# Output projection in two halves, with the next mix maximum's product between them

## The chip, the cores and the metric

The kernel runs on one core of a Trainium2 chip. The metric is the device time of one execution in microseconds (us), lower is better. TensorE (PE) multiplies matrices and has a row of its own for loading weights (PEld), VectorE is DVE, ScalarE is ACT, GpSimd is POOL, and SyncE (SP) issues most of the transfers.

## What is computed

The reference is a backbone of two layers over 2048 latent tokens and 256 context tokens of 1024 features. Each layer makes `mix_x`, the gated outputs of three groups of heads, and then projects it:

```
x_new = x + gate_x[:, None, :] * (mix_x @ w_out[l])
...
ctx = ctx + gate_c * (mix_c @ w_out[l])      # first layer only
x = x_new
...
return rmsnorm(x, norm_f)
```

Each layer begins with an RMSNorm of `x` that is scaled and shifted. The kernel does that of the second layer inside the projection of the first, tile by tile; inside the projection of the second layer it does the final RMSNorm. The change touches only the output projections.

## The kernel before, in words

`mix` lies in device memory. The function `outproj` goes over tiles of 128 tokens, from the last to the first: 18 tiles in the first layer (t from 17 to 0), 16 in the second (t from 15 to 0). A tile is multiplied with `w_out` in float16 pairs: each operand is split into a high part and a low remainder, which makes 24 products for each half of the 1024 outputs, so 48 matmuls of 512 columns per tile (`out_mm`). They go into two PSUM banks, `b_pj` and `b_a`.

To be split, a tile of mix needs its largest absolute value. That takes a chain over four engines:

- `fetch`: SP issues the transfer of the tile into `mx` (two buffers).
- `prep`: DVE takes the maximum along each row (`ms<-mx`), ACT puts it on a diagonal (`dg<-ident,ms`).
- `prepb`: PE multiplies `ones` with that diagonal into a bank `b_b` (`top_b`), so that all partitions see all row maxima. I call it the maximum's product.
- `prep2`: DVE reduces the bank and makes the scale (four short instructions on `ms`), and ACT writes the high part (`m<-mx,ms`; the tile `m2` has two buffers).
- `prep3`: DVE writes the low part (`m<-mx,ms,m`).

What comes out of PSUM goes through `evac` (DVE multiplies the two banks with scale and gate into `xn`, POOL adds `xt`, SP stores the result in the first layer), and through `finish`: ACT sums the squares, POOL makes the power (`rst`), DVE scales (`xh` in the first layer, the output in the second). In the first layer every second tile ends with `put`: PE transposes two tiles of `xh` into banks `b_b` and `b_c`, and ACT, DVE and POOL write the result as `hu` and, split in high and low, as `hx`, the input of the next layer. Also in the first layer, twelve of the steps carry one of four `hooks` that get a block of the next layer's weights ready: load it, take its maximum (DVE, 2.28 us), make its own product on PE, split it (ACT and DVE). `put` stands at the end of the steps t = 15, 13, 11, ... 1, hooks at t = 15, 14, 13, 11, 10, 9, 7, 6, 5, 3, 2, 1.

Every engine but SP runs its part in the order in which the code records it: the class `Pin` (whose line 72 stands for all such instructions in the profile) keeps that order. SP's order is made by a scheduler. So the order of one step of the loop in `outproj` is the order on PE, DVE, ACT and POOL; an instruction that waits holds up all that stand behind it on its engine.

Of the kernel before, what the change touches and what calls it, by code (L numbers as in the profile page):

```python
# [77 lines left out]
def body(ctx: ExitStack, tc: tile.TileContext, a, out, dbg=None):  # L78
    nc = tc.nc
    V, S, G, TE = nc.vector, nc.scalar, nc.gpsimd, nc.tensor  # L80

    def sb(name, bufs=1, side="left"):
        return tc.tile_pool(name=name, bufs=bufs, reuse_waits="tile", side=side)
# [7 lines left out]
    def bank(tag):  # L91
        return ps.tile([P, 512], F32, tag=tag, name="b_" + tag)
# [115 lines left out]
    def rms(pool, xt, junk, S=S, G=G):  # L208
        st = pool.tile([P, 4], F32, tag="rst", name="rst")
        S.activation(out=junk, in_=xt, func=AF.Square, accum_out=st[:, 0:1])  # L210
        G.tensor_scalar(out=st[:, 1:2], in0=st[:, 0:1], scalar1=1.0 / DM, scalar2=EPS, op0=ALU.mult, op1=ALU.add)
        G.tensor_tensor(out=st[:, 2:3], in0=st[:, 1:2], in1=neghalf[:, 0:1], op=ALU.pow)
        return st[:, 2:3]
# [14 lines left out]
    def put_e(pool, l, tiles, pts, V=V, S=S, G=G, hook=None):  # L228
        w2 = 0 if tiles[0] < NL else 1
        t0 = min(tiles) * P  # L230
        for g, pt in enumerate(pts):
            u = pool.tile([P, 2, 256], F32, tag="hu", name="hu", bufs=3)
            for q in range(2):
                kb = 2 * g + q
                src = pt[:, q * 256:(q + 1) * 256]
                if q == 0 or g in PE_A:
                    S.activation(out=u[:, q, :], in_=src, func=AF.Identity, scale=modA[l][:, w2, kb:kb + 1], bias=modS[l][:, w2, kb:kb + 1])
                else:
                    V.tensor_scalar(out=u[:, q, :], in0=src, scalar1=modA[l][:, w2, kb:kb + 1], scalar2=modS[l][:, w2, kb:kb + 1], op0=ALU.mult, op1=ALU.add)
            ks = slice(2 * g, 2 * g + 2)  # L240
            V.tensor_copy(hx[:, 0, ks, t0:t0 + 256], u)
            (G if g < 3 else V).tensor_tensor(out=hx[:, 1, ks, t0:t0 + 256], in0=u, in1=hx[:, 0, ks, t0:t0 + 256], op=ALU.subtract)
            if hook:
                hook(g)
# [1306 lines left out]

        return fetch, prep, prepb, prep2, prep3

    def out_mm(w, t, ms, m2, te=TE):
        pts = [bank("pj"), bank("a")]
        n = 3 * KB
        terms = [(k, mi, wi) for k in range(KB) for mi, wi in ((0, 0), (0, 1), (1, 0))]
        order = [(i, hf) for i in range(n) for hf in range(2)] if t else [(i, hf) for hf in range(2) for i in range(n)]
        for i, hf in order:
            k, mi, wi = terms[i]  # L1560
            te.matmul(out=pts[hf], lhsT=m2[:, mi, k, :], rhs=w[:, wi, k, hf * 512:(hf + 1) * 512], start=(i == 0), stop=(i == n - 1))
        return t, ms, pts

    def outproj(l, last, xin, w, hooks, mid, fetch, prep, prepb, prep2, prep3, ready, mx, done):
        with ExitStack() as st:
            kp = st.enter_context(sb("ok", 1, "right"))
            wk = st.enter_context(sb("owk", 2, "right"))
            gts = kp.tile([P, 2, DM], F32, name="gts")
            nc.sync.dma_start(out=gts.rearrange("p a n -> p (a n)"), in_=gated[l].rearrange("a b -> (a b)").unsqueeze(0).to_broadcast([P, 2 * DM]))
            if last:  # L1570
                nf = kp.tile([P, DM], F32, name="nf")
                nc.sync.dma_start(out=nf, in_=a["norm_f"][0:1, :].to_broadcast([P, DM]))
            held = []
            v, s, g, te = (Pin(tc, e) for e in (V, S, G, TE))

            def fetch_x(t):
                xt = wk.tile([P, DM], F32, tag="xt", name="xt", bufs=4 if last else 3)
                nc.sync.dma_start(out=xt, in_=xin(t))
                return xt

            def evac(t, ms, pts, xt):
                gi = 0 if t < NL else 1
                fast = last and t == 0
                xn = wk.tile([P, DM], F32, tag="xn", name="xn", bufs=3)
                sp = wk.tile([P, 4], F32, tag="sp", name="sp")
                for hf in range(2):
                    sl = slice(hf * 512, (hf + 1) * 512)
                    v.scalar_tensor_tensor(out=xn[:, sl], in0=pts[hf], scalar=ms[:, 4:5], in1=gts[:, gi, sl], op0=ALU.mult, op1=ALU.mult)
                    (v if fast else g).tensor_tensor(out=xn[:, sl], in0=xn[:, sl], in1=xt[:, sl], op=ALU.add)
                    if fast:  # L1590
                        s.activation(out=xt[:, sl], in_=xn[:, sl], func=AF.Square, accum_out=sp[:, hf:hf + 1])
                        v.tensor_tensor(out=xn[:, sl], in0=xn[:, sl], in1=nf[:, sl], op=ALU.mult)
                if not last:
                    nc.sync.dma_start(out=xres[t * P:(t + 1) * P, :], in_=xn)
                return t, xt, xn, sp

            def finish(t, xt, xn, sp):
                if last and t == 0:
                    g.tensor_tensor(out=sp[:, 2:3], in0=sp[:, 0:1], in1=sp[:, 1:2], op=ALU.add)
                    g.tensor_scalar(out=sp[:, 2:3], in0=sp[:, 2:3], scalar1=1.0 / DM, scalar2=EPS, op0=ALU.mult, op1=ALU.add)  # L1600
                    g.tensor_tensor(out=sp[:, 3:4], in0=sp[:, 2:3], in1=neghalf[:, 0:1], op=ALU.pow)
                    r = sp[:, 3:4]
                else:
                    r = rms(wk, xn, xt, S=s, G=g)
                if not last:
                    xh = wk.tile([P, DM], F32, tag="xh", name="xh")
                    v.tensor_scalar_mul(xh, xn, r)
                    held.append((t, xh))
                elif t == 0:
                    v.tensor_scalar_mul(xt[:, 0:512], xn[:, 0:512], r)  # L1610
                    s.activation(out=xt[:, 512:DM], in_=xn[:, 512:DM], func=AF.Copy, scale=r)
                    for sl in (slice(0, 512), slice(512, DM)):
                        nc.sync.dma_start(out=out[t * P:(t + 1) * P, sl], in_=xt[:, sl])
                else:
                    v.scalar_tensor_tensor(out=xt, in0=xn, scalar=r, in1=nf, op0=ALU.mult, op1=ALU.mult)
                    nc.sync.dma_start(out=out[t * P:(t + 1) * P, :], in_=xt)

            def put():
                if len(held) == 2:
                    tiles = [z[0] for z in held]  # L1620
                    put_e(wk, l + 1, tiles, put_t(tiles, [z[1] for z in held], te=te), V=v, S=s, G=g)
                    held.clear()

            ready = [ready]
            prev = None
            for t in range(done[0], -1, -1):
                xt = fetch_x(t)
                cur = out_mm(w, *ready.pop(0), te=te) if prev else done
                if prev:
                    prev = evac(*prev)  # L1630
                if t > 1:
                    z = prep(*mx, V=v, S=s)
                    if t > 2:
                        mx = fetch(t - 3)
                if prev:
                    finish(*prev)
                if t > 1:
                    z = prep2(*prepb(*z, te=te), V=v, S=s)
                if hooks and t < done[0] and t % 4:
                    hooks.pop(0)()  # L1640
                put()
                if t > 1:
                    ready.append(prep3(*z, V=v))
                prev = *cur, xt
            mid()
            finish(*evac(*prev))
            put()

    def xin0(t):
# [7 lines left out]
    with sb("s0", 2, "right") as s0:  # L1657
# [10 lines left out]
        v, s, g, te = (Pin(tc, e) for e in (V, S, G, TE))  # L1668
# [13 lines left out]
        def fetch(i):  # L1682
            if i < len(pairs):
                xs[i] = xt = s0.tile([P, 2, DM], F32, tag="xt", name="xt", bufs=3)
                for q in range(2):
                    tc.keep_in_program_order(nc.sync.dma_start(out=xt[:, q, :], in_=xin0(pairs[i] + q)))
# [25 lines left out]
        pts = []  # L1712
# [35 lines left out]
    for l in range(2):  # L1748
# [56 lines left out]
        v, s = Pin(tc, V), Pin(tc, S)  # L1805
# [12 lines left out]
        def mid():  # L1818
            wst.close()
            if not last:  # L1820
                fst[0] = ExitStack()
                ug[0] = four_pool(fst[0])
                for b in (3, 2):
                    four_x(ug[0], b, nw["fx"])
# [161 lines left out]
```

## Time and profile before

| | |
|---|---|
| median of 3 runs | 2532.82 us (2531.42 to 2536.8) |
| the profiled execution | 2537.43 us, its span 2535.6 us |
| busy share of the span: PE, DVE, ACT, POOL | 92%, 63%, 44%, 44% |
| mean granted clock of TensorE | 0.967 |

A busy share is a mean over the whole span, and the matmuls' records overlap. What the projections cost is read from the stretches in which they run: 1152 to 1386 us for the first layer and 2355 to 2532 us for the second.

### The profile page before, as it was taken

Reading aid. Unit: us, or ns where it says so; the run is one execution under the profiler, and the core shown is the slowest. Engines: PE = TensorE matmul, PEld = TensorE weight load, DVE = VectorE, ACT = ScalarE, POOL = GpSimd, SP = SyncE. Lnnn points to the kernel's source line nnn. Section 1 sums busy time; section 2 is a strip of 40 time slices with the busy share of each in tenths; the row PEclk is TensorE's granted clock in tenths of the full one; section 3 lists DMA queues with packets and bytes.
Section 4 is the critical chain, followed back from the end, with each engine's and each line's share of the span. In section 5 each row is a group of like instructions: output and inputs, shape, how many; then the busy total and the mean of one; then the engine's idle time right before and its main releaser. Section 6 shows DMA issues by size and latency. Waiting matters only on the chain. (4 is left out here: it accounts for less than half of the span.)

```text
span 2535.6 us, 44432 instructions
## 1 busy us (share of the span) xinstructions
PE 2333.9 (92%) x16878; PEld 1554.5 (61%) x16878; DVE 1609.2 (63%) x3607; ACT 1126.5 (44%) x2049; POOL 1117.4 (44%) x1303
## 2 busy tenths in 40 slices
PE   5989998999978999999889999999999699999998
PEld 3555454454546999895444554555555589989444
DVE  5765666666865666695665435667666566669554
ACT  3523554555555444342333224666656434444222
POOL 1534444455544444453334234555555444445232
PEclk7999999999989999999999999999999899999999
DMA  6304124124222100364433021141221210126442
GB/s 250 117 3 131 60 83 123 49 86 121 88 62 66 44 34 35 102 191 154 138 121 110 31 67 49 54 105 55 62 64 34 72 36 35 38 80 200 154 150 100
DMA packets 128298, 225.16 MB, mean 89 GB/s; under 512 B 18346, under 2 KB 81444, under 8 KB 122452
## 3 DMA queue, kind: packets, MB, share of 16 engines
q1 hardware_dynamic: 122900, 212.68, 24.9%
q0 software_dynamic: 5184, 9.64, 2.6%
q8 instruction: 133, 2.18, 0.4%
q14 instruction: 81, 0.66, 0.1%
HBM read 176.89 MB, written 51.47 MB: 90 GB/s over the span
## 5 line engine op out<-in xcount | busy, mean ns | idle before, releaser
L72 PE MATMUL b_pj<-hx,w 128*128 128x512 f16 (+1 forms) x3168 | 690.7, 365 | 0.9 <-DVE w L72 0.9
L72 POOL TENSOR_TENSOR pl<-pt,ph 128x512 f16<-128x512 f32 (+6 forms) x300 | 307.5, 1026 | 433.8 <-ACT ph L72 365.7
L72 PEld LDWEIGHTS <-w 128*128 128x128 f16 x3168 | 305.8, 99 | 276.6 <-issue 15.0
L72 PEld LDWEIGHTS <-hx 128*128 128x128 f16 x5088 | 440.5, 100 | 11.0 <-issue 4.7
L72 PE MATMUL b_pj<-w,hx 128*128 128x192 f16 (+2 forms) x4272 | 396.9, 252 | 4.5 <-DVE zt L72 4.5
L72 PE MATMUL b_pj<-wo,m 128*128 128x512 f16 x816 | 306.2, 384 | 0.0
L72 PE MATMUL b_a<-wo,m 128*128 128x512 f16 x816 | 305.7, 384 | 0.0
L72 PEld LDWEIGHTS <-m 128*128 128x128 f16 x1632 | 161.8, 99 | 190.4 <-issue 9.0
L72 DVE SCALAR_TENSOR_TENSOR pt<-b_a,sc,TS 128x160 f32<-128x160 f32 (+4 forms) x432 | 153.1, 400 | 154.4 <-PE b_a L72 113.6
L72 ACT ACTIVATE pt<-pt,psh 128x480 f32<-128x480 f32 (+1 forms) x192 | 121.7, 634 | 168.2 <-DVE pt L72 158.1
L72 PE MATMUL b_c<-ph,vt 128*128 128x320 f16 (+5 forms) x888 | 179.2, 295 | 0.9 <-ACT ph L72 0.9
L72 PEld LDWEIGHTS <-vt 128*128 128x128 f16 x1332 | 120.8, 100 | 86.2 <-issue 23.2
L72 ACT CAST ph<-pt 128x512 f16<-128x512 f32 (+6 forms) x300 | 166.5, 555 | 9.5
L72 POOL TENSOR_TENSOR xn<-xn,xt 128x512 f32<-128x512 f32 x66 | 82.4, 1270 | 178.0 <-DVE xn L72 178.0
L72 PE MATMUL b_a<-Q,K 128*128 128x320 f16 (+5 forms) x444 | 120.9, 295 | 10.4 <-ACT Q L72 10.2
L72 PE MATMUL b_c<-pl,vt 128*128 128x320 f16 (+5 forms) x444 | 126.9, 295 | 3.6 <-POOL pl L72 3.6
L72 PE MATMUL b_a<-q,k 128*128 128x320 f16 (+5 forms) x444 | 121.6, 295 | 3.5 <-DVE MX L72 1.8
L72 DVE CUSTOM_DVE_ANT_0 b_b<-b_b,tmi 128x512 f32<-128x512 f32 (+3 forms) x144 | 86.5, 601 | 60.0 <-PE b_b L72 58.8
L72 ACT ACTIVATE pt<-b_a,psh,sc 128x512 f32<-128x512 f32 (+1 forms) x108 | 81.0, 750 | 67.1 <-PE b_a L72 61.8
L72 POOL TENSOR_TENSOR hx<-hu,hx 128x512 f16<-128x512 f32 x54 | 69.5, 1302 | 72.6 <-DVE hx L72 72.2
L72 POOL TENSOR_TENSOR ats<-ATm 128x512 f32<-128x512 f32 x34 | 43.3, 1274 | 129.0 <-DVE ATm L72 129.0
L72 PEld LDWEIGHTS <-q 128*128 128x128 f16 x540 | 51.5, 98 | 79.1 <-issue 24.1
(271 smaller groups left out, 4262.7 us busy)
## 6 DMA issues: line engine op xcount, KB each, us to landing
mx<-mixd SPq DMA_DIRECT2D x34, 512.0 KB
ws<-in_w_in SPq DMA_DIRECT2D x16, 1024.0 KB
xt<-in_x SPq DMA_DIRECT2D x32, 512.0 KB
ws<-in_w_ada SPq DMA_DIRECT2D x16, 1024.0 KB
ws<-in_w_out SPq DMA_DIRECT2D x16, 1024.0 KB
TS<-in_ts SPq DMA_DIRECT2D x12, 1000.0 KB
xres<-xn SPq DMA_DIRECT2D x18, 512.0 KB
qdt_d<-qkT SPq DMA_DIRECT2D x34, 256.0 KB
```

Of the source, the lines that this page charges most:

```text
L72: return self.tc.keep_in_program_order(f(*args, **kw))
```

## The change

`out_mm` can now hand back its second 24 matmuls as a function. In a step of `outproj` PE records the first 24, then the maximum's product, then the second 24; before, all 48 stood ahead of the product. The low part of a tile of mix is written one step later, behind `evac` and the row maximum of that step, and the fetch into the freed `mx` buffer follows it. The squares and the power of a norm (`norm_r`) are recorded ahead of the product's reduction, and the scaling (`finish`) behind the second 24 matmuls.

```diff
-    def out_mm(w, t, ms, m2, te=TE):
+    def out_mm(w, t, ms, m2, te=TE, split=False):
         pts = [bank("pj"), bank("a")]
         n = 3 * KB
         terms = [(k, mi, wi) for k in range(KB) for mi, wi in ((0, 0), (0, 1), (1, 0))]
         order = [(i, hf) for i in range(n) for hf in range(2)] if t else [(i, hf) for hf in range(2) for i in range(n)]
-        for i, hf in order:
-            k, mi, wi = terms[i]
-            te.matmul(out=pts[hf], lhsT=m2[:, mi, k, :], rhs=w[:, wi, k, hf * 512:(hf + 1) * 512], start=(i == 0), stop=(i == n - 1))
+        def half(z):
+            for i, hf in order[z * n:(z + 1) * n]:
+                k, mi, wi = terms[i]
+                te.matmul(out=pts[hf], lhsT=m2[:, mi, k, :], rhs=w[:, wi, k, hf * 512:(hf + 1) * 512], start=(i == 0), stop=(i == n - 1))
+
+        half(0)
+        if split:
+            return (t, ms, pts), lambda: half(1)
+        half(1)
         return t, ms, pts
...
-            def finish(t, xt, xn, sp):
+            def norm_r(t, xt, xn, sp):
...
                 else:
                     r = rms(wk, xn, xt, S=s, G=g)
+                return t, xt, xn, r
+
+            def finish(t, xt, xn, r):
...
             ready = [ready]
-            prev = None
+            prev = late = None
             for t in range(done[0], -1, -1):
                 xt = fetch_x(t)
-                cur = out_mm(w, *ready.pop(0), te=te) if prev else done
                 if prev:
+                    cur, more = out_mm(w, *ready.pop(0), te=te, split=True)
                     prev = evac(*prev)
+                else:
+                    cur, more = done, lambda: None
                 if t > 1:
                     z = prep(*mx, V=v, S=s)
-                    if t > 2:
-                        mx = fetch(t - 3)
+                if late:
+                    ready.append(prep3(*late, V=v))
+                    late = None
+                if t > 2:
+                    mx = fetch(t - 3)
+                if prev:
+                    prev = norm_r(*prev)
+                if t > 1:
+                    z = prepb(*z, te=te)
+                more()
+                if t > 1:
+                    late = prep2(*z, V=v, S=s)
                 if prev:
                     finish(*prev)
-                if t > 1:
-                    z = prep2(*prepb(*z, te=te), V=v, S=s)
                 if hooks and t < done[0] and t % 4:
                     hooks.pop(0)()
                 put()
-                if t > 1:
-                    ready.append(prep3(*z, V=v))
                 prev = *cur, xt
             mid()
-            finish(*evac(*prev))
+            finish(*norm_r(*evac(*prev)))
             put()
```

On PE, inside the matmuls of the first layer's tile 16 (`m_12966` is its split mix, `b_b<-dg,ones` the product of a later tile's maximum):

```order
 L72 LDWEIGHTS m_12966
 L72 MATMUL b_a<-wo,m_12966 128x512
+L72 MATMUL b_b<-dg,ones 128x128
 L72 LDWEIGHTS m_12966
 L72 MATMUL b_pj<-wo,m_12966 128x512
```

The product now stands between the tile's 24th and 25th matmul; before, the same row stood behind the 48th.

On DVE, from the end of the first `put` of the first layer (`hx<-hu,hx` is its last instruction) to the reduction of the next product:

```order
 L72 CAST hx<-hu 128x2x256 x2
 L72 TENSOR_TENSOR hx<-hu,hx 128x2x256
-L72 SCALAR_TENSOR_TENSOR m_13645<-mx,ms,m_13645 128x1024
-L72 SCALAR_TENSOR_TENSOR xn<-b_pj,ms,gts 128x512
-L72 SCALAR_TENSOR_TENSOR xn<-b_a,ms,gts 128x512
-L72 TENSOR_REDUCE ms<-mx 128x1
+L72 SCALAR_TENSOR_TENSOR xn<-b_pj,ms,gts 128x512
+L72 SCALAR_TENSOR_TENSOR xn<-b_a,ms,gts 128x512
+L72 TENSOR_REDUCE ms<-mx 128x1
+L72 SCALAR_TENSOR_TENSOR m_13643<-mx,ms,m_13643 128x1024
+L72 TENSOR_REDUCE ms<-b_b 128x1
+L72 TENSOR_SCALAR ms<-ms 128x1
```

The low part of mix moved from ahead of the two evacuations and the row maximum to behind them; `put` stands ahead of both, before and now.

On SP, at the first steps of the first layer's projection (`xres<-xn` is the store of `evac`, `mx` the fetch of a tile of mix, `xt` that of the residual):

```order
+L1600 DMA xres<-xn 128x1024
 L1527 DMA mx<-mixd_88 128x8x128
-L1594 DMA xres<-xn 128x1024
-L1578 DMA xt<-in_x 128x1024 x2
+L1584 DMA xt<-in_x 128x1024
+L1600 DMA xres<-xn 128x1024
 L1527 DMA mx<-mixd_88 128x8x128
```

The store, which waits for POOL, now stands ahead of the fetch of mix in each step.

## Rows read from the trace of the kernel before

**Rows 1.** Waits of the weight loads, first layer's projection: waited for, total us, times, longest

```profile
PEld b_b L72 <- ACT dg L72: 13.3, 6, 4.6
...
PEld b_b L72 <- DVE xh L72: 4.5, 2, 2.9
PEld b_b L72 <- DVE ms L72: 4.1, 2, 2.5
```

**Rows 2.** Waits of PE for a maximum's diagonal, second layer's projection

```profile
PE b_b L72 <- ACT dg L72: 0.9, 1, 0.9
```

**Rows 3.** Windows, the seven from 1187.3 to 1372.2 us: their sum

```profile
sum 184.90, PE 168.90 PEld 85.50 DVE 113.96 ACT 62.27 POOL 71.15; mean PE 24.13 PEld 12.21 DVE 16.28 ACT 8.89 POOL 10.16
```

**Rows 4.** Timeline of weight loads, first layer: start, us, tile, count [idle before <- releaser]

```profile
1176.73 0.41 PEld L72 LDWEIGHTS b_b<-dg,ones 128*128 128x128 f32 x2
...
1187.31 0.41 PEld L72 LDWEIGHTS b_b<-dg,ones 128*128 128x128 f32 x2
1187.63 0.47 PEld L72 LDWEIGHTS b_b<-ident,xh 128*128 128x128 f32 x4
...
1189.38 10.13 PEld L72 LDWEIGHTS <-m 128*128 128x128 f16 x48
1200.05 0.30 PEld L72 LDWEIGHTS b_b<-dg,ones 128*128 128x128 f32 x2 [0.54 <-ACT dg L72]
...
1213.65 0.42 PEld L72 LDWEIGHTS b_b<-ident,xh 128*128 128x128 f32 x4 [2.49 <-DVE ms L72]
...
1254.64 0.30 PEld L72 LDWEIGHTS b_b<-dg,ones 128*128 128x128 f32 x2 [4.58 <-ACT dg L72]
...
1361.49 0.52 PEld L72 LDWEIGHTS b_b<-dg,ones 128*128 128x128 f32 x4 [1.96 <-ACT dg L72]
```

**Rows 5.** Timeline of DVE around the first put

```profile
1187.94 0.29 DVE L72 TENSOR_REDUCE ms<-b_b 128x1 f32<-128x128 f32 x1 [1.21 <-PE b_b L72]
...
1190.43 0.54 DVE L72 TENSOR_SCALAR hu<-b_b,modA,modS 128x256 f32<-128x256 f32 x1 [1.75 <-ACT hu L72]
...
1195.85 1.27 DVE L72 SCALAR_TENSOR_TENSOR m<-mx,ms,m 128x1024 f16<-128x1024 f32 x1
1197.04 0.74 DVE L72 SCALAR_TENSOR_TENSOR xn<-b_pj,ms,gts 128x512 f32<-128x512 f32 x1
...
1198.36 1.20 DVE L72 TENSOR_REDUCE ms<-mx 128x1 f32<-128x1024 f32 x1
1202.49 0.75 DVE L72 TENSOR_SCALAR xh<-xn,rst 128x1024 f32<-128x1024 f32 x1 [2.92 <-POOL rst L72]
```

**Rows 6.** Timeline of ACT around the first put, and a hook's split

```profile
1188.79 1.15 ACT L72 ACTIVATE m<-mx,ms 128x1024 f16<-128x1024 f32 x1 [3.77 <-PE b_c L72]
...
1199.60 0.40 ACT L72 ACTIVATE dg<-ident,ms 128x128 f32<-128x128 f32 x1 [5.76 <-DVE ms L72]
...
1240.31 1.99 ACT L72 ACTIVATE w<-ws,wsm 128x2048 f16<-128x2048 f32 x1
```

**Rows 7.** Timeline of DVE, a hook's split ahead of a put

```profile
1242.33 2.35 DVE L72 SCALAR_TENSOR_TENSOR w<-ws,wsm,w 128x2048 f16<-128x2048 f32 x1 [3.10 <-ACT w L72]
...
1250.44 1.27 DVE L72 SCALAR_TENSOR_TENSOR m<-mx,ms,m 128x1024 f16<-128x1024 f32 x1
```

**Rows 8.** Windows behind waits: length, busy us by engine, PEclk, DMA share, GB/s

```profile
1214.90:1218.40 3.50, 3.50 (x13) 1.92 (x12) 2.54 (x5) 2.45 (x6) 1.55 (x2) 0.51 0.00 0
...
1322.40:1327.70 5.30, 5.28 (x21) 3.95 (x22) 3.07 (x9) 3.62 (x7) 1.88 (x2) 0.52 0.23 83
...
1361.40:1364.00 2.60, 2.51 (x14) 1.44 (x15) 0.09 (x1) 1.19 (x3) 1.13 (x3) 1.00 0.50 202
```

**Rows 9.** Timeline of weight loads, second layer

```profile
2379.39 10.14 PEld L72 LDWEIGHTS <-m 128*128 128x128 f16 x48
```

**Rows 10.** Timeline of SP, second layer: a fetch of mix

```profile
2382.96 0.53 SPq L1527 DMA_DIRECT2D mx<-mixd  x1
```

**Rows 11.** Windows, second layer, behind that fetch

```profile
2387.00:2389.00 2.00, 2.00 (x12) 0.87 (x9) 0.69 (x1) 0.35 (x2) 0.75 (x2) 1.00 0.04 11
```

## The prediction

> **What bounds the kernel now.** I read the list of waits first, for the two stretches in which the projections run. In the first layer's the weight loads stood still for 21.9 us: 13.3 us in six waits for the diagonal of a row maximum, 4.1 us in two for a bank that DVE had not read yet, 4.5 us in two for the normed tile `xh` that `put` transposes [rows 1]. In the second layer's there is one such wait of 0.9 us [rows 2]; the matmuls of a tile follow the last product without a gap [rows 9]. So there TensorE is the limit and the change can gain next to nothing; whatever happens, happens in the first layer.
>
> Next the timeline of the weight loads there. A tile takes 10.58 us from one maximum's product to the next (1176.73 to 1187.31), of which the product has 0.32, so 48 matmuls have 10.26; a `put` adds 1.75 us of transposes (1187.63 to 1189.38) [rows 4]. From the end of tile 15 to the end of tile 1 are seven pairs of tiles. Without any wait they would take 14 x 10.26 = 143.6 for matmuls, 16 x 0.32 = 5.1 for products (13 of mix, 3 of hooks), 7 x 1.75 = 12.3 for transposes: 161.0 us. The windows over them add up to 184.9 [rows 3]. **23.9 us are lost there today**: 19.1 in waits (21.9 less 1.15 that the stretch's first product waits ahead of it and 1.6 of the last `xh` wait behind it; 1.6 is 4.5 less 2.9 [rows 1]), and 4.8 in slow matmuls. For those the windows with the granted clock: behind the waits of 2.49 and 4.58 us, and behind that of up to 2.9 us for `xh`, the clock went to 1.2 GHz (0.51 and 0.52 in the two stretches shown, 3.5 and 5.3 us long); behind a wait of 1.96 us it stayed at 2.4 (1.00) [rows 4, 8].
>
> **The change, part by part.** Nothing is added or removed: the same matmuls, the same DVE, ACT and POOL instructions, the same transfers. So the question is only when each can start. What sets it is DVE behind a `put`: on DVE the put's instructions stand ahead of the next `evac`, the row maximum stands behind `evac`, and the product waits for the diagonal of that maximum. The change leaves that order; it takes one instruction out of the chain, lets the chain start earlier, and moves the point on PE where its result is wanted from the end of the tile to the middle.
>
> *The chain after.* Count from E, the moment at which PE has issued the last matmul of the tile ahead of a put. DVE read the product's bank 0.31 after PE had passed on (1187.63 to 1187.94) [rows 4, 5]; I take 0.31 for ACT's start behind the last matmul too. ACT then writes the high part of mix, which before had to wait for the product and the four short DVE instructions (it began at E + 1.48, 1187.31 to 1188.79 [rows 4, 6]); it still waits for the second 24 matmuls, since `m2` has two buffers and they read the one that it overwrites. From there the spacings are those of before: 1.64 to DVE's first `hu` (1188.79 to 1190.43), 5.42 to the end of the put (to 1195.85), no low part now, 1.32 for the two evacuations (1197.04 to 1198.36), 1.24 to the diagonal (1199.60), 0.45 to the product (1200.05) [rows 4 to 6]. Sum: the product can start at E + 10.38. Before the same sum was 12.74 (1187.31 to 1200.05), of which the low part had 1.19.
>
> *The point where it is wanted.* Before, E + 0.32 + 1.75 + 10.26 = 12.33, and the wait was short (0.54 in the row, 0.41 by this sum). Now E + 1.75 + 5.13 = 6.88. **So the chain got 2.36 us shorter and its deadline 5.45 us earlier: each put is followed by a wait of 10.38 - 6.88 = 3.50 us in the middle of the next tile.**
>
> *With the hooks.* A hook's product behind the second half puts the deadline 0.32 later: 3.18. A hook's maximum puts one more diagonal (at most 0.40 [rows 6]) ahead of `hu`: 3.90. A hook's split ahead of a put takes ACT at most 1.15 for the high part of mix, 2.02 from ACT's start to DVE's (1240.31 to 1242.33), and 8.11 on DVE for split and put (1242.33 to 1250.44) [rows 6, 7]: 0.31 + 1.15 + 2.02 + 8.11 + 3.01 = 14.60, a wait of 7.72. The split of step 6 has no put behind it: 2.69 in place of 8.11 (8.11 - 5.42), 9.18 against 5.13: 4.05. By steps, t = 14, 12, 10, 8, 6, 5, 4, 2: 3.50 + 3.18 + 7.72 + 3.90 + 3.18 + 4.05 + 3.50 + 3.90 = **32.9 us in eight waits**. Behind the put of step 1 there is no product any more.
>
> *The waits that go.* Those for a bank and for `xh` fall away, since the reduction now stands ahead of `xh` and has long been done when `put` begins: `xh` starts 5.45 behind the evacuation (1197.04 to 1202.49) [rows 5], which is while the second half runs. That is in the 23.9 already; the 1.6 behind the last tile's end is saved beside it.
>
> *The clock.* All eight waits are longer than 2.49, so I expect the clock to fall behind nearly all. A fall costs half of 3.3 to 3.5 us [rows 8], some 1.65: 13.2 for eight, 11.6 for seven. Without the clock the change would cost 32.9 - 23.9 - 1.6 = 7.4 us; with it 19 to 20.6. The Trainium skill ("TensorE: Matmul & The Clock Gate", "Why this matters for your kernels") advises against gaps between bursts of matmuls, since they send the clock to its lower level; by that rule the dearer sum holds, and the rows above agree for every wait of 2.49 us or more.
>
> *Parts that I cost at nothing.* The low part one step later: it is wanted a whole tile after it is written, and stands on DVE where DVE waits for the product anyway; without that cover it is 1.19 a tile [rows 5]. The fetch of mix now stands behind the store and the later low part, some 4 us into a tile. That leaves about 8 us to the row maximum of the next (10.58 + 1.6 - 4.1). What SP issued at 2382.96 had landed by 2387 (DMA share 0.04 behind it), so a landing takes 4 us at most [rows 10, 11]. The second layer: evacuation, maximum, diagonal give 0.31 + 1.32 + 1.24 + 0.45 = 3.32 against a half tile of 5.13, 1.8 us to spare, no wait. The hook's products keep their place.
>
> **Sum.** 161.0 + 32.9 + 11.6 for the seven pairs against 184.9, less 1.6: **+19.0 us**, 2556.4 in terms of the profiled execution (2537.43). That run lies 4.6 us above the median of the three, so the time is 2532.8 + 19.0 = **2552 us**.
>
> **The rivals.**
>
> *The clock stays up.* The waits are now short breaks inside a tile, each with 5 us of dense matmuls before and behind. Against it speaks that before the waits of 2.49 and 4.58, too, lay between dense tiles. Then +7.4: 2540.
>
> *Faster.* If the diagonal were ready by the middle of the tile, all of 23.9 + 1.6 is saved: 2507. It decides at E + 6.88: the chain must lose 3.5 of its 10.38 us. For it speaks that the put's 5.42 us hold some waiting for ACT's `hu` and not only work; against it that ACT's part and POOL's buffers are the same as before.
>
> *No change.* Where the chain is some 1 us shorter than I make it, the waits come to about 2.5 us each, the clock mostly holds, and 24 to 26 us of waits replace 25.5 of waits and slow matmuls. 2533.
>
> *Dearer.* The fetch of mix or the store ahead of it is late on SP, and the product waits in the second layer also. 1.8 us are to spare there per tile; each us beyond costs 13. With 1 us the time is 2565. The landing time above speaks against it.
>
> **How the numbers follow.** Chances: forecast 0.64, clock stays up 0.12, faster 0.08, no change 0.07, dearer 0.09. The forecast's own range is 2546 (five falls of the clock, chain 0.3 shorter) to 2557 (eight falls, two at the long wait). For 8 in 10 the range takes in the clock that stays up below and half of the dearer case above: 2537 to 2561. About 0.2%, 5 us, is what a measurement can tell from no change; of the forecast, the clock's rival and the dearer one nearly all lies above it: slower 0.84, same 0.08, faster 0.08.
>
> **What would show it.** In the profile after, the first layer's projection should have some eight waits of `b_b` for the diagonal `dg`, 3 to 4 us each and one near 7.7 at step 10, between the 24th and the 25th matmul of a tile; none for `xh` or for a bank; low granted clock right behind most. DVE should run from the put into the evacuation without a gap. In the second layer nothing should change but places. I am wrong if those waits are under 2 us, which would mean that the put on DVE ends earlier than E + 7.4, or if SP's fetches are waited for.

## The result and the profile after

The changed kernel takes 2556.45 us (median of 4 runs, 2555.36 to 2563.52); the kernel before took 2534.73 us in the same comparison (4 runs, 2531.42 to 2536.8). The ratio is 1.009, its 95% interval 1.0077 to 1.0104: **slower by 21.7 us**, where +19.0 was forecast. The profiled execution took 2556.01 us, its span 2554.2, which is 18.6 over the span before.

The waits of the changed kernel, in three answers: of the weight loads in the first layer's projection, of PE in the second layer's, of SP's queue in the first layer's. The last row is SP's in the kernel before. Columns are total us, times, longest.

```profile
PEld b_b L72 <- ACT dg L72: 34.1, 8, 7.8
PEld L72 <- issue: 17.1, 63, 0.3
...
PE b_b L72 <- ACT dg L72: 0.9, 1, 0.9
...
SPq L1527 <- DVE m L72: 7.4, 11, 0.7
...
SPq L1527 <- DVE m L72: 93.8, 14, 12.3
```

The first row answers to [rows 1]: the waits for a bank (`ms`) and for `xh` are gone, and those for the diagonal went from 12.2 us to 34.1 (the 13.3 of [rows 1] less 1.15 for a wait ahead of the seven pairs; the changed kernel has the same 1.15 us, at 1162.44, and the 34.1 leave it out). The second row is not a wait of the same kind: it is the spacing of matmuls at the low clock, in 63 pieces of 0.3 us. The row of the second layer reads as in [rows 2]. SP's fetch of mix (line 1527) waits less for the low part than before, 0.7 us at most: in SP's order it now follows the store, which waits for POOL. DVE waits for `mx` once, 0.5 us at 1175.25; that is ahead of the seven pairs, and the product that follows, at 1178.31, has no wait.

The timeline of the weight loads shows the place of the eight waits. First the whole of one put and the step behind it; then the seven other waits, the second with one load of the slow stretch behind it and the product that ends it:

```profile
1183.71 0.57 PEld L72 LDWEIGHTS b_b<-ident,xh 128*128 128x128 f32 x4
...
1185.56 4.96 PEld L72 LDWEIGHTS <-m 128*128 128x128 f16 x24
1194.24 0.30 PEld L72 LDWEIGHTS b_b<-dg,ones 128*128 128x128 f32 x2 [3.72 <-ACT dg L72]
1194.45 10.14 PEld L72 LDWEIGHTS <-m 128*128 128x128 f16 x48
1204.71 0.41 PEld L72 LDWEIGHTS b_b<-dg,ones 128*128 128x128 f32 x2
...
1220.59 0.50 PEld L72 LDWEIGHTS b_b<-dg,ones 128*128 128x128 f32 x2 [3.45 <-ACT dg L72]
...
1221.60 0.15 PEld L72 LDWEIGHTS <-m 128*128 128x128 f16 x1 [0.28 <-issue]
...
1232.54 0.41 PEld L72 LDWEIGHTS b_b<-dg,ones 128*128 128x128 f32 x2
...
1252.54 0.50 PEld L72 LDWEIGHTS b_b<-dg,ones 128*128 128x128 f32 x2 [7.79 <-ACT dg L72]
...
1281.74 0.50 PEld L72 LDWEIGHTS b_b<-dg,ones 128*128 128x128 f32 x2 [3.96 <-ACT dg L72]
...
1309.71 0.50 PEld L72 LDWEIGHTS b_b<-dg,ones 128*128 128x128 f32 x2 [3.45 <-ACT dg L72]
...
1327.18 0.50 PEld L72 LDWEIGHTS b_b<-dg,ones 128*128 128x128 f32 x2 [4.14 <-ACT dg L72]
...
1345.74 0.30 PEld L72 LDWEIGHTS b_b<-dg,ones 128*128 128x128 f32 x2 [3.67 <-ACT dg L72]
...
1374.06 0.50 PEld L72 LDWEIGHTS b_b<-dg,ones 128*128 128x128 f32 x2 [3.96 <-ACT dg L72]
...
1391.48 0.57 PEld L72 LDWEIGHTS b_b<-ident,xh 128*128 128x128 f32 x4
```

24 matmuls, then the weight loads stand still for 3.72 us, then come the product and the second 24 together with the next tile's first (PE's own rows, which count from the end of a matmul, have 30.2 us in these eight waits). The transposes at 1183.71 and 1391.48 bound the seven pairs of tiles that [rows 3] bound before: 207.8 us now, 184.9 then, **+22.9**. Ahead of them the changed kernel's profiled run was 3.6 us shorter (1183.71 against 1187.31), behind them 0.7.

The chain that the diagonal waits for, around the first put, in the timeline of all engines (DVE's and ACT's rows, one of POOL, one of SP); it answers to [rows 5, 6]:

```profile
1184.17 1.15 ACT L72 ACTIVATE m<-mx,ms 128x1024 f16<-128x1024 f32 x1 [6.17 <-PE b_a L72]
...
1185.81 0.54 DVE L72 TENSOR_SCALAR hu<-b_b,modA,modS 128x256 f32<-128x256 f32 x1 [5.47 <-ACT hu L72]
...
1191.23 0.74 DVE L72 SCALAR_TENSOR_TENSOR xn<-b_pj,ms,gts 128x512 f32<-128x512 f32 x1
...
1192.04 2.49 POOL L72 TENSOR_TENSOR xn<-xn,xt 128x512 f32<-128x512 f32 x2 [1.29 <-DVE xn L72]
1192.55 1.20 DVE L72 TENSOR_REDUCE ms<-mx 128x1 f32<-128x1024 f32 x1
1193.67 1.94 DVE L72 SCALAR_TENSOR_TENSOR m<-mx,ms,m 128x1024 f16<-128x1024 f32 x1
1193.78 0.40 ACT L72 ACTIVATE dg<-ident,ms 128x128 f32<-128x128 f32 x1 [4.57 <-DVE ms L72]
...
1195.69 0.53 SPq L1527 DMA_DIRECT2D mx<-mixd  x1
```

DVE runs from the put into the evacuation (1191.23) and the row maximum (1192.55) without a gap, and the product follows the diagonal at 1194.24: the chain ends 10.53 us behind E = 1183.71, the end of the tile ahead of the put. The last weight load ended 3.72 us before that.

The windows behind five of the waits; the seventh column of numbers, behind POOL's, is the granted clock as a share of 2.4 GHz:

```profile
1194.50:1198.50 4.00, 4.00 (x21) 1.87 (x21) 3.54 (x7) 1.15 (x2) 0.77 (x3) 1.00 0.65 213
1221.00:1224.00 3.00, 3.00 (x10) 1.22 (x10) 2.30 (x6) 1.06 (x2) 0.74 (x2) 0.56 0.59 209
1252.90:1258.10 5.20, 5.20 (x15) 2.02 (x15) 2.35 (x6) 1.11 (x2) 0.74 (x2) 0.53 0.78 262
1310.10:1316.10 6.00, 6.00 (x17) 2.26 (x17) 2.33 (x6) 1.09 (x2) 0.74 (x2) 0.53 0.78 261
1346.90:1349.90 3.00, 3.00 (x9) 1.04 (x8) 1.55 (x6) 0.31 (x2) 0.74 (x2) 0.50 0.80 266
...
1150.00:1400.00 250.00, 218.59 (x1019) 107.40 (x1020) 147.22 (x233) 73.31 (x120) 86.02 (x91) 0.92 0.35 119
```

Behind the first wait the clock stayed at 2.4 GHz, behind the seven others it stood at 1.2 GHz for a while (in the timeline each is followed by weight loads 0.43 us apart instead of 0.21). So the stretch is 161.0 us of work, 34.1 of waits and a remainder of 207.8 - 161.0 - 34.1 = 12.6 for slow matmuls (counted directly they are more, see below); before, by the same count, it was 161.0 + 19.1 + 4.8.

### The profile page after: what moved, and what is told of

Its sections match the earlier page's. It is cut to its first block, busy times and chain, and to the rows that moved or that the text cites. A ratio compares the mean times of both kernels' runs of the same rounds, so it can differ in the third digit from the quotient of the medians.

```text
span 2554.2 us, 44430 instructions
## 1 busy us (share of the span) xinstructions
PE 2338.1 (92%) x16878; PEld 1555.3 (61%) x16878; DVE 1627.3 (64%) x3607; ACT 1125.3 (44%) x2049; POOL 1119.3 (44%) x1303
## 3 DMA queue, kind: packets, MB, share of 16 engines
q8 instruction: 133, 2.18, 0.3%
## 4 chain that ended last, share of the span: by engine, by line
PE 67%; DVE 19%; ACT 4%; issue 4%; POOL 2%; DMA 2%; SPq 0%; POOLq 0%; ACTq 0%; DVEq 0%
PE b_pj L72 36%; PE b_a L72 13%; PE b_c L72 8%; PE b_b L72 5%; PE b_pj L313 3%; DVE pt L72 2%; DVE ot L72 2%; DVE wsm L72 1%; DVE w L72 1%; DVE b_b L72 1%; DVE b_a L72 1%; DVE hx L72 1%; PE b_a L374 1%; DVE MX L72 1%; DVE wo L72 1%
## 5 line engine op out<-in xcount | busy, mean ns | idle before, releaser
L72 PEld LDWEIGHTS <-w 128*128 128x128 f16 x3168 | 305.1, 98 | 275.5 <-issue 12.9
L72 PEld LDWEIGHTS <-hx 128*128 128x128 f16 x5088 | 440.6, 100 | 11.5 <-issue 5.2
L72 ACT ACTIVATE m<-mx,ms 128x1024 f16<-128x1024 f32 x34 | 39.1, 1149 | 175.3 <-PE b_a L72 167.1
```

The lines of the kernel that those rows point to most:

```text
L72: return self.tc.keep_in_program_order(f(*args, **kw))
```

## The experiments

Times are medians. The first four kernels were compared with 2533.89 us for the kernel before, the last four with 2532.40. The ratios are estimated from all the runs and can differ by 0.001 from the quotients of these medians.

**The product later in the tile.** If the loss is a chain with a fixed end against a point that lies too early, moving the point by 12 matmuls must shorten every wait by 12 x 0.214 = 2.6 us. Two kernels cut the 48 matmuls elsewhere, against the changed kernel (the second has 44 in place of 36):

```diff
+CUT = 36
...
-            for i, hf in order[z * n:(z + 1) * n]:
+            for i, hf in (order[:CUT], order[CUT:])[z]:
```

> The changed kernel with the maximum's product behind the 36th matmul of a tile in place of the 24th; nothing else. Theory: the chain from a put to the next diagonal (10.5 us behind the end of the tile) misses the point on PE where the product stands; 12 matmuls later that point is 2.57 us later. The eight waits of the changed kernel (34.1 us in all) shrink to about 13.6 us (1.1 us where 3.7 stood, 5.2 at step 10), the clock falls behind one only: about 31 us less than the changed kernel, 2525 us, some 10 us under the kernel before. Rival (it costs to break a tile's matmuls, or the later low part and fetch are what is late): the place makes no difference, 2553 to 2559 us.

> As the run with 36, with the product behind the 44th matmul. Theory: the point is 4.28 us later than in the changed kernel; seven of the eight waits go, step 10 keeps about 3.5 us: some 41 us less than the changed kernel, 2515 us, 0.7 to 0.8 per cent under the kernel before. Rival (breaking the tile, low part, fetch): 2553 to 2559 us.

Behind the 36th matmul: **2522.75 us, ratio 0.9947 (0.9929 to 0.9965)**. Behind the 44th: **2517.68 us, 0.9927 (0.9909 to 0.9945)**. The waits of the weight loads with the cut at 36, first layer (one line was added, so 72 reads 73):

```profile
PEld b_b L73 <- ACT dg L73: 14.4, 9, 5.2
...
PEld b_b L73 <- DVE xh L73: 1.7, 2, 1.3
```

and with the cut at 44:

```profile
PEld b_b L73 <- DVE xh L73: 7.6, 8, 1.7
PEld b_b L73 <- ACT dg L73: 5.3, 4, 2.8
```

With the cut at 36, one of the nine waits is 1.15 us ahead of the stretch; the eight behind puts are 1.13, 0.86, 5.21, 1.44, 0.86, 1.55, 0.81 and 1.44. Each is 2.5 to 2.9 us under its partner above (3.72 - 2.57 = 1.15; 7.79 - 2.57 = 5.22). The chain did not move, only the point. With the cut at 44 three waits for the diagonal are left in the stretch (2.75, 0.69 and 0.69; the fourth is the 1.15 ahead), and a small wait for `xh` comes back at each of its seven puts (6.3 us; the other 1.31 of the row belong to the put behind the projection, which waits as long in the changed kernel), since the reduction of a product that ends late stands ahead of `xh` on DVE. The seven pairs take 175.1 us with the cut at 36 and 169.9 at 44 (207.8 at 24).

**The parts alone.** Each of the two main parts was put alone into the kernel before: the cut at 24 with the low part and the norm as before, and the late low part (with the fetch behind it) with all 48 matmuls ahead of the product. The first of them has `out_mm` as in the change; its loop differs so:

```diff
-                cur = out_mm(w, *ready.pop(0), te=te) if prev else done
+                cur, more = out_mm(w, *ready.pop(0), te=te, split=True) if prev else (done, lambda: None)
...
-                    z = prep2(*prepb(*z, te=te), V=v, S=s)
+                    z = prepb(*z, te=te)
+                more()
+                if t > 1:
+                    z = prep2(*z, V=v, S=s)
```

> The kernel before with the product between the two halves of 24 matmuls, and the low part and the norm where they were. Theory: the low part (1.2 us) stays in the chain from the put to the diagonal, so each of the eight waits is 1.2 us longer than in the changed kernel, about 44 us in all: 2566 to 2569 us. Rival (the later low part is what costs): the waits are shorter than in the changed kernel, under 2550 us.

```diff
-                    if t > 2:
-                        mx = fetch(t - 3)
+                if late:
+                    ready.append(prep3(*late, V=v))
+                    late = None
+                if t > 2:
+                    mx = fetch(t - 3)
...
-                    z = prep2(*prepb(*z, te=te), V=v, S=s)
+                    late = prep2(*prepb(*z, te=te), V=v, S=s)
...
-                if t > 1:
-                    ready.append(prep3(*z, V=v))
```

> The kernel before with only the low part, and the fetch behind it, one step later; the 48 matmuls stay whole and the product stands behind them. Theory: the chain loses the low part's 1.2 us at an unchanged deadline, so the waits for the diagonal fall by 1.2 us each and those for a bank and for the normed tile a little: 8 to 11 us less than the kernel before, about 2525 us. Rival (the later low part or fetch is late for somebody): same as before or slower, 2533 us or more.

The cut alone: **2585.2 us, 1.0197 (1.0174 to 1.022)**, dearer than expected. Its waits in the first and then the second layer's projection:

```profile
PEld b_b L72 <- ACT dg L72: 51.0, 16, 9.0
...
PEld b_b L72 <- ACT dg L72: 12.9, 14, 1.5
```

The eight waits behind puts sum to 43.7 us, as expected. What I had missed is the rest: steps without a put wait too, 0.75 to 0.81 us nearly every one, and in the second layer that is every step. The low part stands ahead of `evac` on DVE and waits for ACT's high part, which waits for the second half (two buffers of `m2`). With the terms of the chain that is 0.31 + 1.15 + 1.19 + 3.01 = 5.66 against a half tile of 5.13 (5.81 with the 0.46 that the changed kernel shows for the first term). So the late low part, with the fetch behind it, is worth 2585.2 - 2556.45 = 28.7 us beside the cut at 24; the split of the norm also lies between these two kernels, and the last two runs show it to be worth nothing.

The late low part alone: **2524.49 us, 0.9955 (0.9939 to 0.9971)**, 9.4 us faster than the kernel before, as expected; waits for the diagonal in the first layer fell from 13.3 to 6.8 us (1.31 of the second row belong to the put behind the projection):

```profile
PEld b_b L72 <- ACT dg L72: 6.8, 5, 3.4
...
PEld b_b L72 <- DVE xh L72: 4.9, 3, 2.9
```

**The clock's share.** To tell waiting from slow matmuls, 14 matmuls of 512 columns into an unread bank were added to the changed kernel at seven of the eight waits, between the first half and the product. They are work on top of what the changed kernel does.

```diff
+                    m2 = ready[0][2]
...
+                if t > 1 and not last and t % 2 == 0 and t < 16:
+                    fill = bank("c")
+                    for i in range(14):
+                        te.matmul(out=fill, lhsT=m2[:, 0, 0, :], rhs=w[:, 0, 0, 0:512], start=True, stop=True)
```

> The changed kernel with 14 matmuls of 512 columns (3.0 us of TensorE at full clock) that write a bank nobody reads, in the seven steps behind a put (t = 14, 12, ... 2 of the first layer), between the first 24 matmuls and the maximum's product. They add work and leave nothing out. Theory: they lie in time in which PE waits, so the waits shrink by what they take and the chain of DVE and ACT is untouched; but the clock no longer falls, except at steps 10 and 5 where more than 4 us of wait are left. Of the 12.6 us that slow matmuls cost in the changed kernel about 9 come back: 2547 us, with 21 us more of TensorE work. If the clock's share is less than I make it: 2553 to 2559 us. If PE's time there were not idle: 2577 us.

**2546.64 us, 1.0056 (1.0038 to 1.0073)**: 9.8 us under the changed kernel (8.6 by the two ratios), with more work on PE. The windows of that kernel behind its second and third wait, and over the whole projection:

```profile
1222.70:1226.70 4.00, 4.00 (x21) 1.85 (x19) 2.39 (x6) 1.15 (x2) 0.74 (x2) 1.00 0.68 218
1253.20:1257.20 4.00, 4.00 (x13) 1.47 (x11) 2.36 (x6) 1.12 (x2) 0.74 (x2) 0.57 0.68 222
...
1150.00:1400.00 250.00, 239.50 (x1162) 118.03 (x1163) 148.00 (x236) 74.85 (x123) 90.81 (x96) 0.98 0.36 123
```

Its waits are shorter by the fillers' own time (0.42 us in place of 3.45 at the second, and 14 x 0.214 = 3.0), so that time is neutral; what is saved is clock: 0.98 over 1150 to 1400 us in place of 0.92, and 196.3 us for the seven pairs in place of 207.8. The clock still fell behind the two waits that stayed long (4.78 at step 10, 4.14 at step 5, which had no filler). So 8.6 us (by the ratios) to 11.5 us (by the stretch) of the changed kernel's loss are the clock's, and the two falls that are left hold more. That rules out the rival by which the clock stays up.

**The put away from the deadline.** If DVE's order is the cause, the put's instructions must be able to stand behind the row maximum. Here `put()` moves from the end of a step into the next, behind `prep`; the product stays behind the 24th matmul.

```diff
                 if t > 1:
                     z = prep(*mx, V=v, S=s)
+                put()
...
-                put()
```

> The changed kernel with put recorded one step later, behind the evacuation and the row maximum of the next step: on DVE the put's instructions stand behind the row maximum, on PE its transposes stand between the first 24 matmuls and the product. The product stays in the middle of the tile. Theory: the waits come from DVE's order (put ahead of evacuation and maximum); with the order turned round the diagonal is ready some 3.5 us behind a tile's end, and waits of about 0.3 to 0.5 us a step are left, with 2 to 4 us at the three steps behind a hook's maximum or split: 14 to 18 us lost where the changed kernel loses 47, about 2527 us. Rival (breaking a tile's matmuls costs by itself): 2553 to 2559 us.

**2531.52 us, 0.9993 (0.9983 to 1.0004)**: 25 us under the changed kernel, but only level with the kernel before; I had expected about 2527. Its waits, of the weight loads and, in the last row, of DVE for the fetch of mix:

```profile
PEld b_b L72 <- ACT dg L72: 14.0, 6, 5.2
...
PEld b_b L72 <- DVE hu L72: 4.2, 7, 3.2
...
DVE ms L72 <- DMA mx<-mixd: 6.5, 4, 1.9
```

Behind the puts the wait for the diagonal is gone: all but one of the seven waits for `hu` are 0.16 or 0.22 us, the other, at step 10, is 3.17. Part of that comes from PE's order, since the transposes now stand ahead of the product and put its point off by 1.75 us; that alone would leave waits of 10.53 - 6.88 - 1.75 = 1.9 us, so the rest is DVE's order. But four of the steps that follow wait 1.43 to 2.19 us for the diagonal and one 5.20. Three of the four (at 1232.18, 1284.66 and 1340.49) are the fetch: the low part of mix now stands behind the put, the fetch into the freed buffer behind the low part, and there DVE's row maximum waited 1.36, 1.72 and 1.91 us for that transfer (the fourth wait of the last row, 1.50, is followed by none of PE). The 2.18 at 1207.65 has a hook's maximum (2.28 us) ahead of the evacuation, the 5.20 a hook's split. The order on DVE is the cause of the changed kernel's waits; this other order makes the fetch late, which costs PE 5.4 us in the three waits, about the 4.5 us that are missing to the forecast.

**The norm.** Is the split of power and scaling worth anything? Two kernels scale right behind the power again, one with the cut at 24, one at 44:

```diff
-                    prev = norm_r(*prev)
+                    finish(*norm_r(*prev))
...
-                if prev:
-                    finish(*prev)
```

> The changed kernel, product behind the 24th matmul, with the norm whole again (the scaling ahead of the reduction of the product on DVE). Theory: the scaling and the reduction both lie in the second half of a tile, far from the next put; the split of the norm is worth nothing here: within 3 us of the changed kernel, 2553 to 2559 us. Rival (the split of the norm is part of the loss or holds it down): off by more than 5 us.

> The changed kernel with the product behind the 44th matmul and the norm whole again (the scaling of xh recorded right behind the power, ahead of the reduction of the product). Theory: with the product so late its reduction holds up xh on DVE, which costs 0.5 to 1.7 us at each of eight puts (7.6 us) with the norm split; whole, xh is ready before the tile ends: 6 to 8 us less than the run with 44 alone, about 2511 us. If the split of the norm does nothing there: 2517 us.

With the cut at 24: **2558.21 us, 1.0098 (1.0082 to 1.0115)**, the changed kernel's 1.009 within the intervals. With the cut at 44: **2514.44 us, 0.9928 (0.991 to 0.9946)**, the fastest of all, 18 us under the kernel before and 42 under the changed one. Its waits:

```profile
PEld b_b L73 <- ACT dg L73: 7.4, 5, 3.5
...
PEld b_b L73 <- DVE xh L73: 3.4, 2, 2.1
```

The waits for `xh` fell from 7.6 to 3.4 us as intended, but those for the diagonal rose from 5.3 to 7.4 (with the puts no longer held up, PE reaches the point sooner), and the seven pairs take 169.6 us against 169.9 with the split norm, not 6 to 8 us less as I had expected. The 3 us between the two medians lie outside the stretch, and their ratios to the kernel before, 0.9927 and 0.9928, are the same. So the split of the norm is worth nothing that these runs can tell, at either cut.

## Why the prediction was right

*What is waited for.* "The chain got 2.36 us shorter and its deadline 5.45 us earlier" held. The chain ends at E + 10.53, forecast E + 10.38. All of the difference is in the first term: ACT starts 0.46 behind the last matmul (1183.71 to 1184.17), not 0.31, which I had taken from DVE's start behind a product. From there every spacing is that of before within 0.01: 1.64, 5.42, 1.32, 1.23, 0.46. The two other cuts show the deadline to be the other half of the sum: at 36 it is 6.88 + 2.57 = 9.45, which leaves 10.53 - 9.45 = 1.08, measured 1.13.

*The eight waits.* Forecast 3.50, 3.18, 7.72, 3.90, 3.18, 4.05, 3.50, 3.90, together 32.9; measured 3.72, 3.45, 7.79, 3.96, 3.45, 4.14, 3.67, 3.96, together 34.1, no single one more than 0.27 off. The rows count a little more than is lost: some 0.12 us from the last load to the product stand in a tile without a wait too (the prediction's 0.54 in the row against 0.41 by its sum is the same), and behind a wait at full clock the next loads follow the product 0.1 us sooner (1194.24 to 1194.45, in place of 0.32). Less that, the eight waits lengthen the stretch by about 32.2 us, 0.7 less than the forecast's 32.9.

*The clock.* Seven falls of eight, as forecast, priced 11.6; the remainder gives 12.6, and the filler confirms their cause. Counted fall by fall they cost more: from a product that ends a wait to the next product it is 10.47 us where the clock stayed up (1194.24 to 1204.71) and 11.95 where it fell (1220.59 to 1232.54), and the seven cost 1.5 to 2.9 us each, 14.6 in all, which with 161.0 and 32.2 is the 207.8. So this is the term that was mis-sized, 2.1 a fall in place of 1.65: the prediction took half of two stretches of 3.3 and 3.5 us and left out the one of 5.3 [rows 8]. The two falls that the filler left cost 3.2, and 14.6 - 3.2 = 11.4 is nearly all of its gain of 11.5 in the stretch. The rule of the Trainium skill that the prediction weighed ("TensorE: Matmul & The Clock Gate", "Why this matters for your kernels") agrees with seven of the eight waits, and not with the first, of 3.72 us. That it was seven and not eight is chance, as far as these runs show: the kernel with the norm whole has the same eight waits within 0.01 us, the first of 3.71, and there the clock fell behind all of them (0.50 from 1.0 to 2.5 us behind each).

*The sum for the stretch* was 161.0 + 32.9 + 11.6 - 184.9 = +20.6, measured +22.9: the falls 3.0 more, the waits 0.7 less. One count in it is off without changing it: the stretch before begins with a product (1187.31), so it holds 14 of mix, not 13, and its work is 161.3 where the prediction says 161.0.

*Ahead and behind.* Two sizes were off and offset that in the profiled runs. I gave 1.6 us back behind the last tile. The put there did give back 1.5 (1.85 us from the first transpose to the next matmul in place of 3.38), but all that lies behind the stretch came to 0.7 only. And the changed run reached the stretch 3.6 us earlier, which I had not forecast: 2.1 of it arose ahead of the projection, and 1.5 behind its first tile's start, where the run before had slow matmuls behind a wait of 2.69 us that the run after also has, without them. Neither has to do with the change, as far as the rows show; the kernel with the fillers, whose order is the same up to there, reaches that point at 1185.49, between the two. So 22.9 - 3.6 - 0.7 = +18.6 in the profiled pair, +21.7 on medians. That the first of these lies 0.4 from the forecast's +19.0 is luck; the medians and the +22.9 of the stretch show the forecast's size, 2 to 3 us low.

*What I costed at nothing.* The late low part and fetch: no wait for `mx` in the seven pairs; the low part alone even gains 9.4 us where the cut is left out, and its shorter chain is in the forecast's 2.36. They are near to a cost, though: with the cut at 44 DVE waits for the fetch at four steps, 1.05 to 1.71 us, though PE does not wait for it in turn, and with the put later PE does. The second layer: still one wait of 0.9 us; the cut without the late low part shows how near that was, since 1.19 us more in the chain made every step there wait, 12.9 us in all. The hooks' places: step 10's 7.79 and step 5's 4.14 are where their splits were put.

*The rivals.* "Faster" needed the chain to lose 3.5 us; moving the point by 4.3 us instead (the cut at 44) gave 2518, 11 us above the 2507 of that rival, with 8.9 us of the stretch left over its 161.0. "No change" needed a chain 1 us shorter, and it is 0.15 longer; "dearer" needed waits in the second layer, and they are those of before.

Not settled: when a wait makes the clock fall. Of the changed kernel's eight the first, 3.72 us long, left it up, where 3.45 did not; the kernel before fell behind 2.49, and a wait of 2.75 us in the kernel with the cut at 44 left it up (no slow loads behind it). The length of the wait alone does not decide it.

## What to carry to other kernels

Moving a dependent product into the middle of independent matmuls did not hide its wait here: it moved the point where its input is wanted. Compare the length of the chain (here 10.5 us behind the last matmul) with the work between (6.9 us at half, 11.2 at the 44th of 48), and add to each shortfall what the clock takes behind it (here 1.5 to 2.9 us). Place such a product by that sum, as late as its own successors allow (here 2518 us behind the 44th, 2523 behind the 36th and 2524 behind the 48th with the low part late, though their intervals overlap); and test the parts of a change alone, since here the late low part by itself was a gain that the cut at 24 buried.

## What the runs showed of the hardware

The low part on DVE, one instruction of one shape, became slower by its place alone. Its durations (min/median/max ns) in the first layer's projection, in the kernel before:

```profile
L72 DVE SCALAR_TENSOR_TENSOR m<-mx,ms,m x16: 1271/1274/1286, 1168.7 to 1366.5; 128x1024 f16<-128x1024 f32 x16
```

and in the changed kernel:

```profile
L72 DVE SCALAR_TENSOR_TENSOR m<-mx,ms,m x16: 1352/1943/2039, 1166.9 to 1383.4; 128x1024 f16<-128x1024 f32 x16
```

In the timeline above it starts at 1193.67, while POOL adds `xt` (1192.04 to 1194.53), and it ends 1.08 us behind POOL's end; POOL's pair took 2.49 us. The Trainium skill ("SBUF — State Buffer", "SBUF: two separate sides") says that a DVE instruction with two inputs in SBUF and a GpSimd instruction that reads SBUF exclude each other, the first to start holding the port to its end. An estimate by that page would be 0.86 us of standing still and then 1.27, so 2.13; the trace has 1.94, so it agrees in kind and is 0.2 us shorter. The kernel with the put later has both cases in one trace: 1.95 us where the instruction starts at 1207.08 inside POOL's pair (1205.46 to 1207.95), and 1.27 where it starts at 1231.61 behind it (1228.54 to 1231.04). There it also goes the other way: where the low part starts first (1199.95), POOL's power takes 1.47 us (1200.16) in place of 0.55. The diagonal's product does not wait for this instruction, and what stands behind it on DVE has the time of the second half, so its 0.67 us cost nothing here; where DVE bounds a stretch they would.
